# Seven products instead of eight for the second K chunk's first half in a two-layer encoder trunk

## The chip, the cores and the metric

The kernel runs on one core of one Trainium2 chip. The metric is the device time of one execution in microseconds (us). A timed value is the median of several executions. The profile comes from one further execution; its span, from the first to the last instruction, is a little shorter than that execution's time.

## What is computed

Two encoder layers on an input of 256 positions by 2048 channels, all in float32. Each layer has a mixer (pooling and grouped-query attention in layer 0, a bidirectional matrix-memory mLSTM in layer 1) and a gated feed-forward part, and each part adds its result to the residual x. The feed-forward part is the same in both layers:

```python
def conv_ffn(x, w_up, conv_w, conv_b, w_down):
    u = x @ w_up                                   # 2048 -> 2 * 5632
    up = jnp.pad(u, ((0, 0), (1, 1), (0, 0)))
    u = c[0] * up[:, :-2] + c[1] * up[:, 1:-1] + c[2] * up[:, 2:] + conv_b
    gate, val = jnp.split(u, 2, axis=-1)
    return (jax.nn.silu(gate) * val) @ w_down      # 5632 -> 2048
```

The change touches only the last product, with `w_down`, of layer 0.

## The kernel before, in words

**Precision.** Every float32 operand is split into a high part (rounded to the type F32R) and a low part, the remainder. A product is three matmuls: high by high, high by low and low by high. Weights come from DRAM in chunks of 128 by 1024 values (512 KB). `Stream` (L94 to L159) loads them on the DMA queue of SyncE (SP) into one of six buffers `w`, up to five chunks ahead. `Stream.split` (L124) makes the two parts: ScalarE (ACT) casts the high part (L135), VectorE (DVE) subtracts to get the low part (L136). There are four buffers `hl` for split chunks.

**Feed-forward.** The 44 row tiles of `w_down` (K tiles, 128 rows each) are cut into six K chunks of 4, 8, 8, 8, 8 and 8 tiles (`FCH`, L33). `up` (L993) makes one K tile of the gated activation: 64 matmuls on four weight chunks, then convolution and gate on ACT and DVE. While the tiles of one chunk are made, the `w_down` products of the chunk before it are run, one piece after each `up`; `_ffn_plan` (L1265) writes this order out, and TensorE (PE) keeps it. ACT, DVE, SP and GpSimd (POOL) are put in order by a scheduler when the program is built.

**Eight or seven products.** The 2048 output columns are two halves of two 512-column blocks. In the plain way (`down`, L1133), one call handles one block of 512 columns for all eight K tiles: 48 matmuls of 512 columns and four weight chunks. In the other way (`unit`, L1036), two K tiles, two groups of 128 positions and the two column blocks of a half form a 2 by 2 by 2 product, done in seven products in place of eight, as Strassen and Winograd do. For each pair of K tiles and each half an A unit runs four products (12 matmuls, two chunks) and a B unit three (9 matmuls, one chunk and a half). A unit called with two pairs runs twice that. The partial sums are drained from PSUM on DVE or ACT (`drain`, L1070, L1080 and L1082): four adds after a group of A units, three after a group of B units. A plain block needs two adds (L449).

`BOTH` (L35) lists the chunks for which both halves go the seven-product way. A chunk not in it does so for half 1 only, and half 0 goes through two calls of `down`. In layer 0 that was chunk 1; the last chunk is handled in a way of its own. When one half only is done so, a unit handles one pair; otherwise it handles two. `PASSES` (L39) is the order of the groups.

**Sums of weights.** The A units need four sums of `w_down` blocks for each pair and half. They are made in one of two ways (`_ffn_weights`, L1349):

- `Made`: in DRAM, by `premix` (L476). One mix is ten DMAs: four plain copies on ACT's queue and six that accumulate, on POOL's queue. Each half-tile step waits for the last matmul issued when it was written down (`paced`, L472), so mixes go along with PE. Afterwards the two chunks are loaded by SP like any weights.
- `Sum` and `Chain`: in SBUF. SP loads one chunk, POOL's queue accumulates a second onto it, and DVE makes the other two sums with two adds (L131, L132).

For a chunk that does both halves, even pairs are `Made` and odd pairs are summed in SBUF. For chunk 1 of layer 0 all four pairs of half 1 were summed in SBUF (the second condition of L1350).

**Pacing.** `Weave` (L162) keeps a program clock: each group of matmuls ticks it by its expected length (0.645 for four of `up`, 0.68 for one product). `premix(0, 26.0, 60.0, 8, ...)` (L739), called in the attention stage, starts a mix every 26 ticks up to the eighth, and every 60 afterwards; each takes five times 26 ticks. Two more mixes of layer 0, for the last chunk, are started later and faster (`LATE`, L37 and L1186). There were 16 mixes in layer 0, 14 of them from L739.

Of the kernel before, what the change touches and what calls it, by code (L numbers as in the profile page):

```python
# [31 lines left out]
FT = DFF // P  # L32
FCH = [4, 8, 8, 8, 8, 8]  # L33
CH = 8
BOTH = ((0, 2, 3, 4), (0, 1, 2, 3, 4))  # L35
LAST = (4, 4)
LATE = ((2, 3), (1, 2))  # L37

PASSES = (  # L39
    ("A1 B1 A0 B0", "A1 B1", "A1 B1 A0 B0", "A1 B1 A0 B0", "A0 A1 A1+ B0 B1 B1+"),  # L40
    ("A1 B1 A0 B0", "A1 B1 A0 B0", "A1 B1 A0 B0", "A1 B1 A0 B0", "A0 A1 A1+ B0 B1 B1+"),
)
NEG = -1.0e30
# [50 lines left out]
class Stream:  # L94
# [60 lines left out]
    def next(self):  # L155
        i = self.at
        self.ahead(i)
        self.at += 1
        return self.hl.pop(i)  # L159
# [58 lines left out]
def trunk(ctx: ExitStack, tc: tile.TileContext, gx, xT, xn, call, catt, cml, weights, mixes, out):  # L218
# [253 lines left out]
    def paced(ins):  # L472

        tc.add_manual_dep(ins.ins, last_mm[0].ins.name, now, reason="paced")

    def premix(layer, gap, late, n, which=slice(None)):  # L476

        def one(i, s0, s1, r, made):
            i += which.start or 0
            m = scratch.tile([P, 2, CH * P], F32, tag=f"m{layer}{i}", name=f"m{layer}_{i}")  # L480
            h = CH * P // 2
            steps = [(nc.scalar, m[:, 0], s0, {}), (nc.scalar, m[:, 1], r, {}), (g, m[:, 0], s1, add),
                     (g, m[:, 1, :h], m[:, 0, :h], add), (g, m[:, 1, h:], m[:, 1, :h], add)]
            for n, (eng, to, src, kw) in enumerate(steps):
                for p in range(0, P, P // 2):
                    paced(eng.dma_start(to[p : p + P // 2], src[p : p + P // 2], **kw))  # L486
                    yield (0.1, 0.6, 0.6, 0.6, 0.6)[n] * gap
            for j in range(2):
                made[j].ap = m[:, j]

        for i, e in enumerate(mixes[layer][which]):
            wv.aside(one(i, *e), min(i + 1, n) * gap + max(i + 1 - n, 0) * late)


    def attention_layer(norm, nxt):
        with ExitStack() as es:
# [239 lines left out]
            catb.extend(actp.tile([P, 8, 2, S], F32R, tag=f"B{i}", name=f"cat{i}") for i in range(2))  # L736
            wv.add(k_block(ps))
            wv.tick(0.0)
            premix(0, 26.0, 60.0, 8, slice(0, -LAST[0] // 2))  # L739
            with tc.manual_schedule(engines={mybir.EngineType.SP}):  # L740
                ps = mov_group(xx, "qproj0", after=squares)
            wv.add(q_block(ps, 0, 5.5))
# [447 lines left out]
    norms = [Norm(0), None]  # L1190
    norms[1] = Norm(1)
    attention_layer(norms[0], norms[1])
    norms.append(Norm(2))
    ffn_layer(0, norms[1], norms[2])
# [55 lines left out]
def _halves(layer, c):  # L1250

    return () if c == len(FCH) - 1 else (0, 1) if c in BOTH[layer] else (1,)

# [6 lines left out]
def _direct(layer, c, b):  # L1260

    return LAST[layer] if c == len(FCH) - 1 and b >= NB // 2 else 0


def _ffn_plan(layer):  # L1265

    slots, late, units = [[] for _ in range(FT)], [], []
    at = 1
    for c in range(len(FCH) - 1):
        at = max(at + (c == 0) * FCH[0], sum(FCH[: c + 1]))
        step = len(_halves(layer, c))
        for pas in PASSES[layer][c].split():
            k = c + pas.endswith("+")
            for j in range(0, _pairs(layer, k), step):
                units.append((pas[0], k, int(pas[1]), tuple(range(j, j + step))))
                to = slots[min(at, FT - 1)] if at <= FT else late  # L1280
                to.append(len(units) - 1)
                if step == 1 and pas[0] == "A" and j % 2:
                    to.append(("down", c, j // 2))
                at += 1
    for n, u in enumerate(units):
        first, last = (not 0 <= m < len(units) or (units[m][0], units[m][2]) != (u[0], u[2]) for m in (n - 1, n + 1))
        units[n] = u[:4] + (first, last, all(o[2] != u[2] for o in units[n + 1 :]))
    slots = [[e if isinstance(e, tuple) else units[e] for e in slot] for slot in slots]

    busy = {(u[1], j): f for f, slot in enumerate(slots) for u in slot if u[0] == "A" for j in u[3]}  # L1290
    seq, f0 = [], 0
    for c, n in enumerate(FCH):
        for i in range(n):
            seq.append(("up", c, i))
            mixes = [(busy.get((c - 1, j), 0) - f0, ("mix", c, j)) for j in range(_pairs(layer, c))]
            mixes = [(k, e) for k, e in mixes if i == max(2 * e[2] + 1, k)]

            soon = [e for k, e in mixes if c == len(FCH) - 1 and k < i]
            seq += soon + slots[f0 + i] + [e for _, e in mixes if e not in soon]
        f0 += n  # L1300
    seq += [("two", c, 0)] + [units[e] for e in late] + [("two", c, 1)]
    return seq + [("down", c, b) for b in range(2, NB)]
# [27 lines left out]
def _ffn_weights(layer, up, parts):  # L1330

    down = iter(parts[0])
    out, u, mixes = [], 0, []
    for kind, c, i, *j in _ffn_plan(layer):
        if kind == "up":
            out += up[u : u + 4]
            u += 4
        elif kind in ("down", "two"):
            n = FCH[c] // 2 - 1
            out += [next(down) for _ in range((n, n + 2)[i] if kind == "two" else (FCH[c] - _direct(layer, c, i)) // 2)]  # L1340
        elif kind != "mix":
            q0 = sum(FCH[:c]) // 2
            s0, s1, r, ba, bb = parts[1 + 5 * i : 6 + 5 * i]
            js = [q0 + e for e in j[0]]
            if kind == "B":
                last = bb[js[0] // 2]
                out += [ba[q] for q in js] + [last if len(js) == 2 else last[:, js[0] % 2 * 512 : js[0] % 2 * 512 + 512]]
                continue
            for q in js:  # L1349
                if c < len(FCH) - 1 and (q % 2 or i and c == 1 and layer == 0):  # L1350
                    out += [Sum(s0[q], s1[q]), Chain(r[q])]
                else:
                    made = [Made(), Made()]
                    mixes.append((s0[q], s1[q], r[q], made))
                    out += made
    return out, mixes
# [103 lines left out]
```

## Time and profile before

| what | value |
|---|---|
| median of 3 executions | 2159.14 us (2157.9 to 2159.89) |
| the profiled execution's own time | 2158.39 us |
| its span | 2156.6 us |
| granted TensorE clock, mean | 1.000 |
| feed-forward part of layer 0 in the span | about 263 to 967 us |
| stretch in which chunk 1 of layer 0 is multiplied by `w_down` | about 437 to 553 us |

"Busy" counts the time in which an engine has an instruction under way; for PE the ends of matmuls are modelled, so that PE at 100% may still run below its best. The DMA share is the busy time of packets over that of the 16 DMA engines. It can be somewhat over 1, where packets of several queues overlap on one engine.

### The profile page before, as it was taken

To read this page: it belongs to the slowest core of one execution; us is meant where nothing else is said; L and a number is where in the kernel's file an instruction comes from. 1 tells how busy PE (TensorE), PEld (TensorE's weight loads), DVE (VectorE), ACT (ScalarE), POOL (GpSimd) and SP (SyncE) were. 2 spreads that over 40 slices of the span, in tenths; PEclk is the share of its full clock that TensorE was granted. 3 is DMA by queue.
4 is the path that set the end of the run, shared out by engine and by line. 5 is a ranking of instruction groups with operands and counts; after the bars stand their busy time and mean duration, and the time that the engine had idled before them with its cause. 6 is when DMAs were issued, how large, how long until landed. Compare 5 with 4: busy or idle time off the path is not lost.

```text
span 2156.6 us, 32025 instructions
## 1 busy us (share of the span) xinstructions
PE 2150.5 (100%) x11400; PEld 1844.0 (86%) x11400; DVE 1746.3 (81%) x2451; ACT 1419.9 (66%) x2222; POOL 231.8 (11%) x294
## 2 busy tenths in 40 slices
PE   9999999999999999999999999999999999999999
PEld 7888888888888888889888888888888888888887
DVE  7686678887988899897777676667888998989988
ACT  7665577766777777766454544457777777777774
POOL 0022111110011110001111111111100000000000
PEclk9999999999999999999999999999999999999999
DMA  9668989897999897779887888988978988878775
GB/s 327 211 205 244 290 240 310 253 283 240 301 311 319 278 311 237 262 268 240 232 256 241 246 246 232 275 268 250 282 241 271 306 273 274 289 249 271 237 249 195
DMA packets 168164, 566.78 MB, mean 263 GB/s; under 512 B 21339, under 2 KB 23939, under 8 KB 168003
## 3 DMA queue, kind: packets, MB, share of 16 engines
q1 hardware_dynamic: 130496, 465.96, 61.5%
q0 software_dynamic: 22624, 56.90, 15.9%
q10 hardware_dynamic: 14882, 41.86, 6.0%
q8 instruction: 89, 1.46, 0.3%
q14 instruction: 73, 0.59, 0.1%
HBM read 562.51 MB, written 77.64 MB: 297 GB/s over the span
## 4 chain that ended last, share of the span: by engine, by line
PE 98%; DVE 1%; DMA 0%; issue 0%; ACT 0%; DVEq 0%
PE up L273 45%; PE pp L273 16%; PE op L273 8%; PE mv L273 4%; PE mq L273 4%; PE mk L273 4%; PE mo L273 4%; PE dn L273 4%; PE qproj L273 3%; PE vproj L273 1%; PE kproj L273 1%; PE pool L273 1%; PE av L273 1%; PE qk L273 1%; PE xt L324 0%; DVE hl L136 0%
## 5 line engine op out<-in xcount | busy, mean ns | idle before, releaser
L136 DVE TENSOR_TENSOR hl<-w,hl 128x1024 fp32r<-128x1024 f32 (+1 forms) x846 | 1017.0, 1214 | 212.0 <-ACT hl L135 209.4
L135 ACT CAST hl<-w 128x1024 fp32r<-128x1024 f32 (+1 forms) x845 | 867.0, 1045 | 429.4 <-PE up L273 123.1
L273 PE MATMUL up<-xx,hl 128*128 128x512 f32 (+1 forms) x5632 | 993.8, 337 | 0.0
L273 PEld LDWEIGHTS up<-xx,hl 128*128 128x128 f32 x5632 | 867.4, 188 | 129.8 <-DVE hl L136 0.4
L273 PE MATMUL pp<-hl,s 128*128 128x512 f32 x864 | 214.7, 390 | 0.1
L486 POOL DMA_DIRECT2D m<-m x144 | 116.4, 811 | 728.5 <-PE up L273 293.7
L273 PEld LDWEIGHTS pp<-hl,s 128*128 128x128 f32 x864 | 159.2, 188 | 31.9 <-DVE hl L136 0.9
L273 PE MATMUL pp<-hl,g 128*128 128x512 f32 x648 | 165.1, 390 | 0.0
L273 PEld LDWEIGHTS pp<-hl,g 128*128 128x128 f32 x648 | 119.1, 188 | 22.9
L439 ACT COPY tb_up<-up 128x512 f32<-128x512 f32 x88 | 51.7, 587 | 124.3 <-PE up L273 124.2
L486 POOL DMA_DIRECT2D m<-in_dn x72 | 60.9, 846 | 478.8 <-PE dn L273 149.1
L1005 DVE TENSOR_TENSOR y<-y,z 128x510 f32<-128x510 f32 x88 | 60.7, 690 | 60.3 <-ACT y L1004 60.2
L1004 ACT ACTIVATE y<-tb_up,conv 128x256 f32<-128x256 f32 x176 | 103.8, 590 | 0.0
L440 DVE TENSOR_TENSOR tb_up<-up,tb_up 128x512 f32<-128x512 f32 x88 | 60.8, 691 | 40.5 <-ACT tb_up L439 40.3
L273 PE MATMUL mk<-xx,hl 128*128 128x512 f32 (+1 forms) x512 | 92.2, 337 | 0.0
L273 PE MATMUL mq<-xx,hl 128*128 128x512 f32 (+1 forms) x512 | 92.2, 338 | 0.0
L273 PE MATMUL mv<-hl,xx 128*128 128x512 f32 (+2 forms) x480 | 91.8, 351 | 0.0
L273 PE MATMUL op<-hl,cat 128*128 128x512 f32 x384 | 91.6, 393 | 0.0
L1002 ACT ACTIVATE z<-tb_up,conv 128x256 f32<-128x256 f32 x176 | 88.5, 503 | 3.1 <-DVE tb_up L997 2.8
L273 PE MATMUL mo<-hl,xx 128*128 128x512 f32 x384 | 90.5, 391 | 0.0
L273 PE MATMUL op<-hl,mcat 128*128 128x512 f32 x384 | 89.5, 392 | 0.0
L273 PEld LDWEIGHTS mq<-xx,hl 128*128 128x128 f32 x512 | 79.3, 188 | 11.6
(233 smaller groups left out, 2180.0 us busy)
## 6 DMA issues: line engine op xcount, KB each, us to landing
w<-in_up SPq DMA_DIRECT2D x352, 512.0 KB, 5.2
w<-in_dn SPq DMA_DIRECT2D x174, 512.0 KB, 4.9
w<-in_m_in SPq DMA_DIRECT2D x124, 512.0 KB, 5.3
m<-in_dn ACTq DMA_DIRECT2D x144, 256.0 KB, 5.8
w<-m SPq DMA_DIRECT2D x72, 512.0 KB, 4.9
w<-in_a_in SPq DMA_DIRECT2D x46, 512.0 KB, 4.5
m<-in_dn POOLq DMA_DIRECT2D x72, 256.0 KB, 6.8
m<-m POOLq DMA_DIRECT2D x144, 128.0 KB, 5.4
```

Source lines behind the costliest of these rows:

```text
L135: (self.nc.vector.tensor_copy if i + c == 0 else self.nc.scalar.copy)(hl[:, 0, c : c + n], w[:, c : c + n])
L136: low = self.nc.vector.tensor_sub(hl[:, 1, c : c + n], w[:, c : c + n], hl[:, 0, c : c + n].bitcast(F32))
L273: last_mm[0] = pe.matmul(out_, lhsT, rhs, start=start, stop=stop, skip_group_check=True)
L439: a.copy(tb, ps[:, :, 1, :])
L440: v.tensor_add(tb, ps[:, :, 0, :], tb)
L486: paced(eng.dma_start(to[p : p + P // 2], src[p : p + P // 2], **kw))
L1002: a.activation(z[:, 0, j, :], u[:, j, :], AF.Copy, scale=cw(tl, 0))
L1004: a.activation(y[:, j, :], u[:, j, :], AF.Identity, scale=cw(tl, 1), bias=cw(tl, 3))
L1005: v.tensor_add(y[:, :, 1:S], y[:, :, 1:S], z[:, 0, :, 0 : S - 1])
```

## The change

Chunk 1 of layer 0 is put into `BOTH`: both its halves take seven products, and its units take two pairs at a time. Its even pairs' sums now come from DRAM and its odd pairs' from SBUF, as in the other chunks. This makes four further mixes in L739's list (18 there, 20 in layer 0), and they are placed ahead of those of chunk 2, so that the mixes of chunks 2 to 4 move back by four places. From the ninth mix on, one is started every 34 ticks instead of every 60.

```diff
-BOTH = ((0, 2, 3, 4), (0, 1, 2, 3, 4))
+BOTH = ((0, 1, 2, 3, 4), (0, 1, 2, 3, 4))
...
 PASSES = (
-    ("A1 B1 A0 B0", "A1 B1", "A1 B1 A0 B0", "A1 B1 A0 B0", "A0 A1 A1+ B0 B1 B1+"),
+    ("A1 B1 A0 B0", "A1 B1 A0 B0", "A1 B1 A0 B0", "A1 B1 A0 B0", "A0 A1 A1+ B0 B1 B1+"),
...
-            premix(0, 26.0, 60.0, 8, slice(0, -LAST[0] // 2))
+            premix(0, 26.0, 34.0, 8, slice(0, -LAST[0] // 2))
...
-                if c < len(FCH) - 1 and (q % 2 or i and c == 1 and layer == 0):
+                if q % 2 and c < len(FCH) - 1:
                     out += [Sum(s0[q], s1[q]), Chain(r[q])]
```

Around chunk 1 the order on PE becomes, after each `up` of chunk 2 (before: one pair of A or B, and after the second and the fourth a plain block):

```
A half 1 pairs 0,1 | A half 1 pairs 2,3 | B half 1 pairs 0,1 | B half 1 pairs 2,3
A half 0 pairs 0,1 | A half 0 pairs 2,3 | B half 0 pairs 0,1 | B half 0 pairs 2,3
```

## The prediction, made before the changed kernel ran

> **What bounds the kernel now.** I read the shares of the engines and the chain of waits on the page first, then the chain piece by piece, then busy time by stretch.
>
> ```profile
> span 2156.6 us, 32025 instructions
> ...
> PE 2150.5 (100%) x11400; PEld 1844.0 (86%) x11400; DVE 1746.3 (81%) x2451; ACT 1419.9 (66%) x2222; POOL 231.8 (11%) x294
> ...
> PE 98%; DVE 1%; DMA 0%; issue 0%; ACT 0%; DVEq 0%
> ```
>
> PE is the bound from end to end. A busy PE need not be at its best, so the pace has to be read from equal pieces of work. In the chain in order of time (start, length, what):
>
> ```profile
> 425.69 11.13 PE up L273 x64
> ...
> 439.56 10.88 PE dn L273 x48
> ...
> 478.17 10.88 PE dn L273 x48
> ...
> 500.19 2.05 PE pp L273 x9
> ...
> 552.93 5.45 PE pp L273 x24
> ...
> 586.11 4.09 PE pp L273 x18
> ...
> 653.82 11.14 PE up L273 x64
> ...
> 669.05 11.35 PE up L273 x64
> ```
>
> Each `up` takes 11.13 or 11.14 us, in chunk 1's stretch (one half in seven products) and in chunk 2's (both halves, from 552.93). A matmul of 512 columns takes 5.45 / 24 = 0.227 us everywhere. One piece is late, the `up` at 669.05, by 11.35 - 11.14 = 0.21 us. So removed matmuls are removed time, and what has to be asked is whether weights still come in time.
>
> ```profile
> 289.00:427.00 138.00, 138.00 (x765) 119.48 (x764) 117.68 (x163) 103.43 (x171) 20.63 (x26) 1.00 0.89 270
> 427.00:553.00 126.00, 126.00 (x674) 108.27 (x673) 103.13 (x136) 83.12 (x131) 12.03 (x15) 1.00 0.87 268
> 553.00:680.00 127.00, 127.00 (x678) 108.89 (x677) 113.26 (x150) 92.97 (x141) 16.87 (x21) 1.00 0.96 309
> 680.00:807.00 127.00, 127.00 (x680) 109.20 (x679) 114.97 (x152) 92.55 (x140) 15.35 (x19) 1.00 0.94 298
> ```
>
> The columns are PE, PEld, DVE, ACT and POOL busy (instructions), clock, DMA share and GB/s. Chunk 1 (second row) has room on every unit; chunks 2 and 3 show a stage with both halves in seven products: DVE at 90%, the DMA engines at 0.94 to 0.96, PE undisturbed but for 0.21 us.
>
> **PE's saving.** Half 0 of chunk 1 costs two plain blocks, 2 x 10.88 = 21.76 us. In seven products it costs two double A units and two double B units, 2 x 5.45 + 2 x 4.09 = 19.08 us. That is 12 matmuls fewer; 12 x 0.227 = **-2.73 us** is the term I use. Half 1 keeps its matmuls; its single units become double ones.
>
> **Vector work, covered.**
>
> ```profile
> L136 DVE TENSOR_TENSOR hl<-w,hl 128x1024 fp32r<-128x1024 f32 x832 | 1006.1, 1221 | 210.7 <-ACT hl L135 208.0
> ...
> L135 ACT CAST hl<-w 128x1024 fp32r<-128x1024 f32 x832 | 857.6, 1050 | 422.8 <-PE up L273 121.2 <-PE op L273 62.5 <-PE mo L273 32.0
> ...
> L1082 DVE TENSOR_TENSOR acc<-acc,pp 128x512 f32<-128x512 f32 x60 | 39.7, 681 | 0.0
> ...
> L449 DVE TENSOR_TENSOR x<-x,dn 128x512 f32<-128x512 f32 x18 | 11.6, 680 | 0.0
> ...
> L136 DVE TENSOR_TENSOR hl<-w,hl 128x512 fp32r<-128x512 f32 x8 | 5.4, 688 | 1.3 <-ACT hl L135 1.3
> ...
> L135 ACT CAST hl<-w 128x512 fp32r<-128x512 f32 x7 | 4.3, 621 | 4.0 <-PE up L273 2.0 <-issue 1.5 <-DMA w<-in_a_in 0.4
> ```
>
> Chunks of chunk 1 to be split: before, half 0 had 8 whole ones, half 1 had 12 whole and 4 half-wide (a single B unit loads half a chunk). After, each half has 14 whole. That is 8 whole more and 4 half-wide fewer. DVE: 8 x 1.221 - 4 x 0.688 = 7.0 us, and 7 drains in place of 4 plain adds, 7 x 0.681 - 4 x 0.680 = 2.0 us: +9.1 us. The adds of `Chain` stay, since four pairs are summed in SBUF before and after. DVE comes to (103.13 + 9.1) / 123.3 = 91% of chunk 1's stretch, and chunk 3 has 114.97 / 127 = 90.5% with PE undisturbed: I cost it at nothing. Without that cover at most the excess over chunk 3's share, some 0.6 us, would show. ACT gets 8 x 1.050 - 4 x 0.621 = 5.9 us and 16 issues of DMAs:
>
> ```profile
> L486 ACTq DMA_DIRECT2D m<-in_dn x144: 497/498/617, 58.3 to 1820.4; - x144
> L486 POOL DMA_DIRECT2D m<-m x144: 772/778/1438, 155.3 to 1868.3; - x144
> ```
>
> 16 x 0.5 = 8 us on ACT and 24 x 0.78 = 19 us on POOL, over the 500 us in which mixes run. ACT stays under 80% and POOL under 20%: nothing.
>
> **Are the sums from DRAM there in time?** A load of a sum that isn't ready would hold SP's queue, every weight load behind it, and then PE. The first eight mixes start at the same ticks as before, 26 apart, so this trace tells when they are done, whoever uses them. Chunk 1's four are now the third to the sixth.
>
> ```profile
> 364.67 0.86 POOL L121 DMA_DIRECT2D sum<-in_dn  x1 [6.58 <-DMA sum<-in_dn]
> ...
> 385.64 0.78 POOL L486 DMA_DIRECT2D m<-in_dn  x1 [4.80 <-PE up L273]
> ```
>
> In POOL's built order of before, the sixth mix's last step stands ahead of the accumulation at 364.67 and the seventh's ahead of the one at 385.64; in the built order after, the sixth's has the same place and the seventh's stands two places later. Chunk 1's products begin at 436.8, its half 0 some 60 us later, chunk 2's at 552.93. The last of L739's list ended at 208 + 6 x 60 + 130 = 698 ticks and now ends at 208 + 10 x 34 + 130 = 678, for the same unit of chunk 4. So no step is late by its pacing, and I cost this at nothing.
>
> **The DMA engines: the open cost.**
>
> ```profile
> q1 hardware_dynamic: 130496, 465.96, 61.5%
> q0 software_dynamic: 22624, 56.90, 15.9%
> q10 hardware_dynamic: 14882, 41.86, 6.0%
> ...
> w<-in_up SPq DMA_DIRECT2D x352, 512.0 KB, 5.2
> ...
> m<-in_dn ACTq DMA_DIRECT2D x144, 256.0 KB, 5.8
> ...
> m<-in_dn POOLq DMA_DIRECT2D x72, 256.0 KB, 6.8
> m<-m POOLq DMA_DIRECT2D x144, 128.0 KB, 5.4
> ```
>
> In time of all 16 engines, a MB costs 0.615 x 2156.6 / 465.96 = 2.85 us on SP's queue (q1), 3.09 on ACT's (q10) and 6.03 on POOL's (q0). A mix moves 4 x 256 KB on ACT's and 2 x 256 KB + 4 x 128 KB on POOL's queue, 1.05 MB on each: 3.24 + 6.32 = 9.56 us. A weight chunk is 0.524 MB, 1.49 us. The change adds four mixes (38.2 us) and the equal of 28 - 22 = 6 chunks (8.9 us). Where does it fall? A slot of `up` and a double A unit ticks 16 x 0.645 + 8 x 0.68 = 15.76 in 11.13 + 5.45 = 16.58 us, so 60 ticks are 63.1 us and 34 are 35.8. From the ninth mix on, mixes take 9.56 / 35.8 = 0.267 of the engines, not 9.56 / 63.1 = 0.151: +0.116. Chunk 1's chunks add 8.9 / 126 = 0.07. The stretches become 0.87 + 0.116 + 0.07 = **1.06** and 0.96 + 0.116 = **1.08**; the other 9 us lie about them (0.89 to some 0.93, 0.94 to 0.97). How full can they get? Stretches of 25 us:
>
> ```profile
> 0.00:25.00 25.00, 23.40 (x91) 18.88 (x92) 18.60 (x37) 18.12 (x29) 0.73 (x9) 1.00 0.95 368
> 200.00:225.00 25.00, 25.00 (x119) 20.71 (x118) 15.17 (x20) 13.94 (x24) 4.81 (x6) 1.00 1.05 317
> 350.00:375.00 25.00, 25.00 (x137) 21.55 (x136) 22.83 (x30) 17.96 (x29) 4.03 (x5) 1.00 1.02 315
> 625.00:650.00 25.00, 25.00 (x138) 21.58 (x137) 23.19 (x33) 16.90 (x27) 4.08 (x5) 1.00 1.03 336
> 650.00:675.00 25.00, 25.00 (x133) 21.20 (x132) 20.26 (x28) 19.58 (x32) 5.48 (x7) 1.00 1.00 328
> ```
>
> 1.05 is the most. The two rows at 625 to 675, at 1.03 and 1.00, end in the one late `up`. There ACT waited for weights, in the list of waits of 553 to 807:
>
> ```profile
> ACT hl L135 <- DMA w<-in_up: 4.6, 5, 2.6
> ```
>
> So the engines, now full in spots, would be full for some 250 us. The cost from both sides: nothing, if it is as at 350 to 375 (full, no late piece); 0.06 x 126 + 0.08 x 127 = 17.7 us, if all above 1.00 delays PE. A share counts waiting within a packet too: 0.95 moved 368 GB/s in the first row, where 0.87 moved 268 at chunk 1, so that sums of shares overstate. I take the nearest row, 0.21 us lost in 50 us at 1.00 to 1.03, for 253 us: 1.06, say **+1.0 us**.
>
> **The sum.** -2.73 + 1.0 = -1.7 us: 2158.39 becomes 2156.7 in the profiled execution (its span lies 1.8 below its time). The median of the runs is 0.75 above that execution, so the forecast for the median is **2157.4 us**, -0.08%. About 0.2% (4.3 us) is what a measurement of this kernel can tell from no change; the whole saving on PE, 0.13%, is below it.
>
> **The rivals.**
>
> *Everything is hidden.* The shares overstate the load; PE runs as evenly as in chunk 3's stretch. For: 350 to 375. Against: 669.05. 2159.1 - 2.7 = 2156.4.
>
> *The gain is eaten.* The engines hold 1.05 over the whole stretch, as at 200 to 225, and the rest delays PE: 0.01 x 126 + 0.03 x 127 = 5.1 us, 2161.5.
>
> *Slower: weights late in the stretch from 427 to 680.* Accumulating DMAs and weight loads share the engines. If they hold only what 625 to 650 shows, 1.03, the rest is 0.03 x 126 + 0.05 x 127 = 10.1 us, 2166.5. It decides against the change from a lost 2.73 us on, and shows as slower by over 0.2% from 7.1 us on, at a ceiling of about 1.04. The worst place is from 616 on, where the first of the two fast late mixes runs beside the others. For: 0.21 us there already. Against: the late mix runs in that place now as well, and mixes are paced by PE, so that they wait when PE does. The Trainium skill, in HBM Reference, Specifications (TRN2), gives about 358 GB/s for a core; by it, an estimate from 309 GB/s and 25 more for the denser mixes, with the mixes' writes to DRAM counted as well, the stage of chunk 2 would already be over the limit. This trace speaks against so low a limit: its first row moved 368 GB/s. The same skill, in DMA: Bandwidth & Descriptors, Issuing engines are not separate DMA queues, says that the transfers of all queues interleave on the same 16 engines; by that the loads do pay for the mixes, and the rows at 625 to 675 agree.
>
> *The change does something else.* The scheduler may place DVE's and ACT's work otherwise and remove more than it costs. There is little to remove: 0.21 us in this part. For over 0.2% faster, -4.3 us, something outside the steps above would have to move.
>
> **How the numbers follow.** Forecast (0.5 to 2.5 us lost) 0.46; everything hidden 0.18; gain eaten (2.5 to 7 us lost) 0.14; slower 0.18, at 2166.5 or beyond in half of it; something else, faster, 0.04. The first three lie within 0.2%: same 0.78, slower 0.18, faster 0.04. The range goes from everything hidden less 1 us of scatter (the three runs span 2.0 us), 2155.4, to 2164.5, which takes in the eaten gain and the lower part of the slower case; some 0.14 is left out above and 0.04 below.
>
> **What would show it.** In the chain after, chunk 1's stretch should have no `dn` of 48 matmuls, four pieces of 5.45 and four of 4.09, and `up` at 11.14; the start of chunk 3's products should be 2.7 us earlier less what was lost. The DMA share from 427 to 680 should be 1.0 or over. If `up` pieces are longer there and ACT's L135 waits for DMA, the slower rival holds; if they wait for L136 instead, my cover on DVE was wrong. If SP waits for a DMA of a mix, the lateness that I cost at nothing was wrong. A share well under 1.0 would make my sum of shares wrong.

## The result and the profile after

| kernel | median | lowest to highest | ratio to before, 95% interval |
|---|---|---|---|
| before | 2159.14 us | 2157.9 to 2160.58, 7 runs | |
| changed | 2165.8 us | 2162.3 to 2170.32, 7 runs | 1.0032 [1.0022, 1.0042] |

The changed kernel is slower by 6.7 us, and its runs scatter over 8 us where those of before scatter over 2.7. With the 2.73 us that PE was to save, 6.7 + 2.7 = 9.4 us are lost in a median run. The profiled execution is the fastest of the seven, 2162.30 us against 2158.39 before; it lost 3.9 + 2.7 = 6.6 us. So the trace shows a mild case; where the slower runs lost the rest isn't recorded.

The page of the changed kernel, the span, the busy times and the chain by engine:

```profile
span 2160.5 us, 32121 instructions
...
PE 2150.2 (100%) x11388; PEld 1840.7 (85%) x11388; DVE 1754.6 (81%) x2458; ACT 1426.3 (66%) x2226; POOL 250.7 (12%) x318
...
PE 95%; DVE 3%; DMA 1%; issue 1%; ACT 0%; ACTq 0%; DVEq 0%
```

There are 12 matmuls fewer, and PE is on the chain for 95%, not 98%: DVE, DMA and issue (time in which the profile shows no wait) have got in. The same stretches as in the prediction (columns PE, PEld, DVE, ACT, POOL busy, clock, DMA share, GB/s):

```profile
289.00:427.00 138.00, 138.00 (x762) 119.05 (x761) 117.52 (x164) 104.35 (x173) 22.85 (x29) 1.00 0.91 284
427.00:553.00 126.00, 126.00 (x676) 108.27 (x675) 112.86 (x146) 91.16 (x137) 20.32 (x26) 1.00 0.99 322
553.00:680.00 127.00, 122.96 (x650) 103.65 (x649) 107.49 (x141) 89.24 (x135) 22.98 (x29) 1.00 1.01 321
680.00:807.00 127.00, 126.17 (x674) 108.07 (x674) 114.59 (x151) 92.05 (x140) 17.64 (x22) 1.00 0.94 299
```

In chunk 1's own stretch, the second row, PE is busy all the time. PE idles in the third row, 127.00 - 122.96 = 4.0 us, and a little in the fourth. The chain in order of time (start, length, what):

```profile
423.09 5.45 PE pp L273 x24
428.54 11.15 PE up L273 x64
...
508.78 11.14 PE up L273 x64
...
538.69 0.49 ACT y L1004
...
554.87 9.27 DMA w<-in_dn
...
574.64 11.14 PE up L273 x64
...
652.26 15.48 DMA w<-in_dn
...
667.82 1.06 ACT hl L135
668.90 1.24 DVE hl L136
...
671.62 0.43 ACTq L486
...
687.47 1.23 DVE hl L136
...
690.17 11.14 PE up L273 x64
```

Up to 535 the pieces are as short as before, and the plain blocks of 10.88 us are gone. Then the chain leaves PE three times. From 538.69 it runs over ACT and DVE to the load of a weight chunk, 9.27 us at 554.87, and returns over DVE. From 649 it goes to a second load, 15.48 us at 652.26, and returns through the cast on ACT and the subtraction on DVE. The third time, from 671.62 to 688.75, it stays on ACT and DVE and there is no load in it. The list of waits from 553 to 700 shows the side of those who wait (in total, times, longest):

```profile
ACT hl L135 <- DMA w<-in_dn: 8.9, 5, 2.5
DVE w L131 <- DMA w<-in_dn: 6.2, 3, 4.7
PEld pp L273 <- DVE hl L136: 5.8, 5, 1.3
ACT hl L135 <- DMA w<-in_up: 5.1, 7, 1.1
```

The worst place is where the first fast late mix runs beside the others, 616 to 680. Queues (packets, MB, share) and loads (count, size, median us to landing) there, before:

```profile
q0 software_dynamic: 1166, 3.01, 25.5%
...
w<-in_up SPq DMA_DIRECT2D x16, 512.0 KB, 8.0
w<-in_dn SPq DMA_DIRECT2D x8, 512.0 KB, 9.2
```

and in the changed kernel:

```profile
q0 software_dynamic: 1411, 3.63, 31.2%
...
w<-in_up SPq DMA_DIRECT2D x15, 512.0 KB, 10.7
w<-in_dn SPq DMA_DIRECT2D x8, 512.0 KB, 9.1
```

POOL's accumulating queue takes 31% of the engines for 3.63 MB, and the loads for `up` land 2.7 us later at the median; those for `dn` don't, 9.1 us against 9.2. PE waits for L136, and L136 in its turn stands behind chunks that came late. Whether late chunks or DVE's own work start this, the trace alone can't tell: DVE is on the chain for 3%, the loads for 1%. The experiments have to.

### The profile page after: what moved, and what is told of

Same layout as the page of the kernel before. It is cut to its first block, busy times and chain, and to the rows that moved or that the text cites. A ratio compares the mean times of both kernels' runs of the same rounds, so it can differ in the third digit from the quotient of the medians.

```text
span 2160.5 us, 32121 instructions
## 1 busy us (share of the span) xinstructions
PE 2150.2 (100%) x11388; PEld 1840.7 (85%) x11388; DVE 1754.6 (81%) x2458; ACT 1426.3 (66%) x2226; POOL 250.7 (12%) x318
## 3 DMA queue, kind: packets, MB, share of 16 engines
HBM read 574.04 MB, written 86.03 MB: 306 GB/s over the span
## 4 chain that ended last, share of the span: by engine, by line
PE 95%; DVE 3%; DMA 1%; issue 1%; ACT 0%; ACTq 0%; DVEq 0%
PE up L273 43%; PE pp L273 16%; PE op L273 8%; PE mv L273 4%; PE mq L273 4%; PE mk L273 4%; PE mo L273 4%; PE qproj L273 3%; PE dn L273 3%; DVE hl L136 1%; DMA w<-in_dn 1%; PE kproj L273 1%; PE vproj L273 1%; PE pool L273 1%; PE av L273 1%
## 5 line engine op out<-in xcount | busy, mean ns | idle before, releaser
L136 DVE TENSOR_TENSOR hl<-w,hl 128x1024 fp32r<-128x1024 f32 (+1 forms) x850 | 1023.2, 1216 | 205.0 <-ACT hl L135 201.7
L273 PE MATMUL pp<-hl,s 128*128 128x512 f32 x912 | 227.5, 390 | 3.3 <-DVE hl L136 3.2
L486 POOL DMA_DIRECT2D m<-m x160 | 129.6, 815 | 796.0 <-PE up L273 319.4
L273 PEld LDWEIGHTS pp<-hl,s 128*128 128x128 f32 x912 | 167.9, 188 | 38.6 <-DVE hl L136 5.7
L273 PE MATMUL pp<-hl,g 128*128 128x512 f32 x684 | 174.5, 390 | 1.1 <-DVE hl L136 0.8
L273 PEld LDWEIGHTS pp<-hl,g 128*128 128x128 f32 x684 | 125.8, 188 | 26.2 <-DVE hl L136 1.1
L486 POOL DMA_DIRECT2D m<-in_dn x80 | 68.6, 859 | 404.2 <-PE dn L273 137.2
```

What stands on the lines that cost most here:

```text
L136: low = self.nc.vector.tensor_sub(hl[:, 1, c : c + n], w[:, c : c + n], hl[:, 0, c : c + n].bitcast(F32))
L273: last_mm[0] = pe.matmul(out_, lhsT, rhs, start=start, stop=stop, skip_group_check=True)
```

## The experiments

Two theories were set against each other. TRAFFIC: the 16 DMA engines are too full with mixes, so weight loads land late. VECTOR: DVE has too much to split and to drain. All times are medians; "lost" is the difference to the kernel before as timed along with that run, plus 2.73 us where half 0 of chunk 1 is done in seven products.

| run | seven products for both halves | mixes | median, us | ratio, 95% interval | lost, us |
|---|---|---|---|---|---|
| changed | yes | 20, every 34 | 2165.8 | 1.0032 [1.0022, 1.0042] | 9.4 |
| e1 | no | as changed, 4 unread | 2169.47 | 1.0049 [1.0036, 1.0061] | 10.5 |
| e2 | yes, sums in SBUF | as before | 2159.24 | 1.0000 [0.9991, 1.0009] | 3.0 |
| e3 | yes | earlier | 2159.3 | 1.0003 [0.9994, 1.0012] | 3.1 |
| e4 | no | 16, every 34 | 2160.33 | 1.0006 [0.9998, 1.0015] | 1.4 |
| e5 | yes | first late one slower | 2160.97 | 1.0012 [1.0003, 1.0021] | 4.7 |
| e6 | yes | earlier, none late | 2157.04 | 0.9991 [0.9982, 1.0000] | 0.8 |
| e7 | no | e1, unread ones plain | 2169.86 | 1.0052 [1.0038, 1.0066] | 10.9 |
| e8 | yes | still earlier, none late | 2156.42 | 0.9990 [0.9981, 0.9999] | 0.2 |
| e9 | no | e1, unread ones at 515 to 740 us | 2169.3 | 1.0046 [1.0033, 1.0059] | 10.2 |
| e10 | no | e9, unread ones plain | 2163.55 | 1.0019 [1.0010, 1.0028] | 4.5 |
| e11 | no | e8's | 2159.86 | 1.0007 [0.9998, 1.0016] | 0.8 |
| e12 | yes | every 34, none late | 2161.89 | 1.0014 [1.0005, 1.0023] | 5.5 |

### e1: the mixes without the products

```diff
-            premix(0, 26.0, 60.0, 8, slice(0, -LAST[0] // 2))
+            premix(0, 26.0, 34.0, 8, slice(0, -LAST[0] // 2))
...
+        if l == 0:
+            m[2:2] = [e[:3] + ([Made(), Made()],) for e in m[2:6]]
         mixes.append(m)
```

> The kernel before (plain blocks for half 0 of chunk 1, four pairs of half 1 summed in SBUF) with the changed kernel's mixes: four further mixes of which nobody reads the result, in the same four places of the list, and one mix every 34 ticks from the ninth on. The result is the reference's. TRAFFIC theory (the 16 DMA engines are too full with mixes, weight loads land late): the loss of the changed kernel without its gain. That loss is 2165.8 - 2159.1 + 2.7 = 9.4 us, so about 2168 us, 2164 to 2171. VECTOR theory (the further splits and drains on DVE make the split chunks late): DVE's work is that of before, so 2158.5 to 2160 us.

2169.47 us: the loss without the gain, 10.5 us, about 1 us more than the 9.4 of the changed kernel. DVE had no more to do than before. VECTOR falls as the main cause; TRAFFIC holds. The stretch 616 to 680 of this run:

```profile
616.00:680.00 64.00, 59.76 (x308) 49.17 (x307) 50.12 (x66) 42.01 (x66) 12.15 (x15) 1.00 1.02 319
```

PE is missing 4.2 us in it, and DVE, with 50.12 of 64 us, is less busy than in the same stretch before (57.34) and in the changed kernel (53.41): it waits as well.

### e2: the products without further mixes

The further condition for chunk 1 is widened to both its halves, and the pacing is that of before.

```diff
-                if q % 2 and c < len(FCH) - 1:
+                if c < len(FCH) - 1 and (q % 2 or c == 1 and layer == 0):
```

> The changed kernel with seven products for both halves of chunk 1, but all its pairs summed in SBUF, so no further mixes, and 60 ticks between mixes as before. TRAFFIC theory: the mixes' load is that of before, so most of the 2.7 us is kept: 2156 to 2158 us. VECTOR theory: DVE has the changed kernel's splits and drains and 8 more adds of 0.68 us, 5.5 us, which makes it 95% of chunk 1's stretch: as late as the changed kernel or later, 2165 us or more.

2159.24 us, between the two: 6.6 us better than the changed kernel, and yet the 2.73 us are eaten. DVE got 8 more adds than in the changed kernel, so VECTOR's 2165 us and more are refuted; TRAFFIC's 2156 to 2158 us are missed too. The chain of this run from 480 to 530, and two of its waits from 490 to 530, show waits behind which the rest can have gone:

```profile
490.46 9.09 DMA sum<-in_dn
...
512.46 12.07 DMA w<-in_up
```

```profile
POOL sum L121 <- DMA sum<-in_dn: 17.4, 3, 8.3
...
DVE w L131 <- DMA sum<-in_dn: 3.5, 1, 3.5
```

A sum in SBUF is two transfers one after the other into one of three buffers. With eight such pairs in chunk 1, DVE waits 3.5 us for one of them, and behind this wait stand the splits of the chunks that PE needs. So this variant pays, at least in part, in lateness of its own sums; a weight load, 12.07 us at 512.46, is on its chain as well, and the two weren't separated.

### e3: mixes in the attention stage

```diff
-            premix(0, 26.0, 34.0, 8, slice(0, -LAST[0] // 2))
+            premix(0, 20.0, 42.0, 10, slice(0, -LAST[0] // 2))
```

> The changed kernel with its mixes moved to the attention stage, where the DMA share is 0.53 to 0.80 from 75 to 200 us: a mix every 20 ticks for the first ten, every 42 afterwards (before the edit 26 for eight, then 34). TRAFFIC theory: mixes take 9.56 / 44 = 0.22 of the engines from 400 us on instead of 0.27, and end some 40 us earlier: the loss falls from 9.4 us to 2 to 6 us, 2158.5 to 2162.5 us. VECTOR theory: DVE's work is unchanged: 2164 to 2167 us.

2159.3 us: 6.3 of the 9.4 us come back by moving the same DMAs, with DVE's work unchanged.

### e4: the kernel before with denser mixes

> The kernel before with one edit, 34 ticks in place of 60 between its 14 mixes: as many mixes as before, denser from about 290 us on and ended at 542 ticks, some 590 us, so ahead of the fast late mix at 616 us. TRAFFIC theory: shares of 0.98 to 1.08 up to 590 us, less afterwards: 0 to 3 us lost, 2159 to 2162 us; if it is the amount of mixes together with the late mix that costs, nothing is lost. VECTOR theory: 2159 us.

Its edit is the first of e1's. 2160.33 us, an interval that holds 1. Its list of mixes ended later than the 590 us expected: the last step was issued on POOL at 623.56 us, the first POOL step of the late mix at 642.96. So a dense stretch ahead of the late mix costs little, and the four mixes more, which carry the density on through the late mix, come with the other 9 us of e1.

### e5 and e12: the late mix

e5 gives the first late mix 24 ticks in place of 12. e12 takes the late ones out of their place and sets them at the end of the list.

```diff
-LATE = ((2, 3), (1, 2))
+LATE = ((), (1, 2))
...
-            premix(0, 26.0, 34.0, 8, slice(0, -LAST[0] // 2))
+            premix(0, 26.0, 34.0, 8)
```

> The changed kernel with one edit: the first of the two late mixes, which starts at about 616 us, takes 5 x 24 ticks in place of 5 x 12. TRAFFIC theory, with the late mix as the place that matters (PE's losses of the profiled executions lie at 640 to 690 us for the greater part): the late mix's share falls from 0.15 to 0.075 of the engines there, and some 5 of the 9.4 us lost come back: 2159.5 to 2163 us. TRAFFIC theory without that (the density from 427 to 680 us alone matters): 2164.5 to 2167 us.

> The changed kernel with one edit: no late mixes, its two last ones stand at the end of the list instead, at the unchanged 26 and 34 ticks. TRAFFIC theory with the late mix as the place that matters most: as e5_late_mix_slower or a little better, 2158.5 to 2161 us, with what is lost at 565 to 575 us left over. If moving mixes into the attention stage is what counts: 2164 us or more.

2160.97 us and 2161.89 us: about half of the loss, 4.7 and 3.9 us, is the late mix's. e12 came out 0.9 us above its range, with 5.5 us still lost: what is left without the late mix is more than I had allowed for.

### e6 and e8: earlier and none late

e6 is e12 with `premix(0, 20.0, 40.0, 10)`, e8 with `premix(0, 18.0, 46.0, 12)`.

> The changed kernel with all 20 mixes of layer 0 in the list that starts in the attention stage (no late ones), a mix every 20 ticks for the first ten and every 40 afterwards. TRAFFIC theory: mixes take 9.56 / 42 = 0.23 of the engines, evenly, with nothing fast on top at 616 us, and the loss falls to 0 to 1.5 us: 2156.3 to 2158 us, faster than the kernel before. If density alone matters and not the late mix, as e3_mixes_earlier: 2159 to 2160 us.

> e6_earlier_no_late with a mix every 18 ticks for the first twelve and every 46 afterwards: 9.56 / 48 = 0.20 of the engines after some 330 us, at the price of 0.50 before. TRAFFIC theory: 2156.3 to 2157.5 us, no later than e6_earlier_no_late, unless the attention stage, denser now, loses something itself (PE's pieces from 100 to 260 us would show it).

2157.04 and 2156.42 us. e8 keeps 2.6 of the 2.73 us and is the fastest of all kernels here, 0.1% below the one before, with an interval that leaves out 1 only just. Four kernels, with the late mix in place or not and the list early or not, make a table of what is lost: late mix, list not early 9.4 (changed); no late mix, list not early 5.5 (e12); late mix, list early 3.1 (e3); no late mix, list early 0.8 (e6, which has 40 ticks where e3 has 42). e8's stretch from 616 to 680 and its chain:

```profile
616.00:680.00 64.00, 64.00 (x343) 54.97 (x343) 58.48 (x78) 46.91 (x72) 8.07 (x10) 1.00 0.97 309
```

```profile
428.47 11.15 PE up L273 x64
...
572.35 11.14 PE up L273 x64
...
651.20 11.14 PE up L273 x64
...
666.43 11.14 PE up L273 x64
677.56 5.45 PE pp L273 x24
683.01 11.13 PE up L273 x64
...
730.05 11.13 PE up L273 x64
```

PE is undisturbed at a share of 0.97, with DVE at 58.48 / 64 = 91%. So DVE, at the load that the prediction called covered, is covered. This profiled execution, 2155.15 us, is the fastest of its eleven.

### e11: e8's pacing on the kernel before

> The kernel before with e8_earlier_sparser's pacing alone: all 16 mixes from the attention stage on, every 18 ticks for twelve, then every 46, none late. TRAFFIC theory: the kernel before lost 0.21 us to the late mix and nothing else, so there is nothing to gain: 2158.5 to 2159.5 us, and e8_earlier_sparser's 2.6 us are those of the 12 matmuls. If earlier mixes gain something by themselves: 2156 to 2158 us.

2159.86 us, an interval that holds 1 and a median 0.4 us above its range: the pacing gains nothing by itself, so e8's gain is that of the 12 matmuls. In its trace PE is missing 1.75 us from 289 to 427, where e8 at the same pace misses nothing; why isn't known.

### e7, e9 and e10: does accumulation count?

e7 is e1 with the four unread mixes' accumulations made plain copies. e9 is e1 with the unread mixes 13th to 16th in the list (`m[12:12]` in place of `m[2:2]`); e10 is e9 with theirs made plain.

```diff
-        def one(i, s0, s1, r, made):
+        def one(i, s0, s1, r, made, add=add):
...
-            m[12:12] = [e[:3] + ([Made(), Made()],) for e in m[2:6]]
+            m[12:12] = [e[:3] + ([Made(), Made()], {}) for e in m[2:6]]
```

> e1_traffic_only with the four unread mixes' accumulating DMAs made plain copies: the same ten DMAs, queues and bytes, no addition (what they write is read by nobody; the result is the reference's). If it is the engines' time that counts, and accumulation is what makes a MB on POOL's queue cost 6.03 us and not about 3, a mix costs 6.5 us and not 9.56, and the loss falls from 10.5 to 3 to 6 us: 2162 to 2165 us. If bytes, or the number of DMAs on the queues, count: 2168 to 2171 us as e1_traffic_only.

> As e1_traffic_only, the kernel before with the changed kernel's rate of mixes, but the four unread mixes stand 13th to 16th in the list, so that their own DMAs run from about 515 to 740 us, where PE's losses lie, and not before 370 us. TRAFFIC theory: the same DMAs run at the same times, only for other data, so as e1_traffic_only: 2168 to 2171 us.

> e9_traffic_in_place with the accumulating DMAs of the four unread mixes made plain copies (nobody reads what they write). If it is engine time that counts and accumulation costs 6.03 us a MB where a plain copy costs about 3, the mixes of 515 to 740 us load the engines by 0.18 in place of 0.27, and most of the 10.5 us lost comes back: 2160 to 2164 us. If bytes or the number of DMAs count: 2168 to 2171 us, as e9.

e7, 2169.86 us against 2162 to 2165 expected, looks as if accumulation cost nothing. But it was set up badly: the third to sixth mixes run before 370 us, where PE loses nothing, so what is saved on them can't come back. Its trace does give the price. From 160 to 270 us, POOL's queue in e1 and then in e7:

```profile
q0 software_dynamic: 1872, 4.85, 25.3%
```

```profile
q0 software_dynamic: 1744, 4.85, 19.1%
```

The same MB take a quarter less of the engines' time when part of them is copied and not added.

e9 and e10 put them where the losses are: 2169.3 and 2163.55 us. The same DMAs with the same bytes on the same queues, without the addition, give back 5.7 of 10.2 us. In the stretch 616 to 680, e9 first, then e10:

```profile
q0 software_dynamic: 1396, 3.62, 32.4%
...
w<-in_up SPq DMA_DIRECT2D x13, 512.0 KB, 12.0
w<-in_dn SPq DMA_DIRECT2D x8, 512.0 KB, 12.9
```

```profile
q0 software_dynamic: 1182, 3.50, 25.6%
...
w<-in_up SPq DMA_DIRECT2D x14, 512.0 KB, 10.7
w<-in_dn SPq DMA_DIRECT2D x8, 512.0 KB, 10.7
```

About as many MB take 32.4% or 25.6% of the engines, and the weights land 1.3 to 2.2 us earlier. So it is the engines' time that counts, more than the bytes that the profile counts.

## Why the prediction was wrong

**What bounds the kernel; PE's saving: right.** The plain blocks are gone, the pieces measure 5.45 and 4.09 us, and the medians of e8 and before differ by 2.58 of the 2.73 us. The chain shows it without that scatter: the same `up` begins at 653.82 us before and at 651.20 in e8, 2.62 us earlier.

**Vector work, covered: right.** DVE did 112.86 of 126 us in chunk 1's stretch, 90% (91% forecast), with PE undisturbed there. e1 and e8 settle that this work isn't the main cause: the loss comes without DVE's further work, and it goes with that work in place.

**Sums there in time: right.** The profile after shows PE's delays behind weights from `in_dn` and `in_up`; ACT's waits for loads of mixes are 0.5 us where those for `in_dn` are 8.9. SP, whose wait for a mix was to be the sign of lateness, waits 1.1 us for DMAs of mixes in the first 1000 us, and 2.8 us before the change.

**The DMA engines: the step that failed.** The mechanism was the one named, and so was the worst place, from 616 on: the engines are full, and weights come late. It stood as the rival with a chance of 0.18 and 2166.5 us, and the median is 2165.8. What failed is the size of the term: "I take the nearest row, 0.21 us lost in 50 us at 1.00 to 1.03, for 253 us: 1.06, say +1.0 us". Measured, the term is 9.4 us.

The loss was taken to grow with the length of the full stretch. It doesn't. Set beside the same `up` pieces in e8, those of the changed kernel begin 0.1 us later at 428.54, 2.3 us later at 574.64, and 7.2 us later at 690.17 as well as at 737.22. So the profiled execution loses in two short places: 2.2 us ahead of 575, and 4.9 us from 638 to 690. Nor does the share say where: at 0.99 PE was missing nothing from 427 to 553, and at the same 0.99 it was missing 1.6 us from 553 to 616 (the third row of the table above, in two parts):

```profile
553.00:616.00 63.00, 61.40 (x329) 52.13 (x328) 54.08 (x71) 43.60 (x66) 10.09 (x13) 1.00 0.99 312
616.00:680.00 64.00, 61.55 (x324) 51.52 (x323) 53.41 (x71) 45.64 (x69) 12.88 (x16) 1.00 1.03 330
```

The second place is the late mix's. The term treated the stretch as one, though this mix takes 9.56 us of the engines' time in some 64 us there, before the change as well, and now on top of the denser mixes. In the trace of e5, where it takes twice as long, the 4.9 us are 1.0, and in that of e12, where it isn't in this place, 2.3. The first place is left in these two, with 3.1 and 3.2 us, and it needs more than mixes: e1 and e9, which have the mixes without the further chunks of chunk 1, lose about 1 us there, and e8, which has these chunks without the dense mixes, loses nothing. Whether it is the loads of these chunks or their splits that meet the mixes there wasn't separated.

That the rival's 2166.5 us came so near is partly luck. Its 10.1 us were what a sum of shares has above 1.03, spread over both stretches, 3.8 us of it in chunk 1's. Nor were its signs as I had given them: the `up` pieces kept their 11.14 us and the products were late, and PE's waits for L136 stand beside ACT's for DMAs, so that the two signs didn't tell the theories apart. e1 did.

The sums of shares, 1.06 and 1.08, came out as 0.99 and 1.01: they did overstate, as the prediction said, and I drew comfort from that. But the share says little once it is near 1. No 25 us of before have more than 1.05, and the same 1.03 from 616 to 680 goes with 2.5 us of missing PE time in the changed kernel and 4.9 in e9. What differs is the landing times. For the loads of `up` and of `dn` in this stretch they are 6.0 and 7.1 us in e8, where nothing is lost, 8.0 and 9.2 before, with one piece 0.21 us late, 10.7 and 9.1 in the changed kernel, and 12.0 and 12.9 in e9. The trace of before had them: 5.2 us for `in_up` over the span, and 8.0 from 616 to 680. That row is the best sign there was of how little was left, and the prediction didn't use it. That the loss sets in once the split chunks kept ready are used up fits this, but no run measured how many were left.

The Trainium skill's statement that the transfers of all queues interleave on the same engines (DMA: Bandwidth & Descriptors, Issuing engines are not separate DMA queues) is borne out by e1: four mixes that nobody reads, on other queues than the weights', bring 9 of its 10.5 us (e4, the same without them, loses 1.4).

The Trainium skill gives some 358 GB/s for a core in HBM Reference, Specifications (TRN2), and says there that a core streaming alone measures well above this share. The trace agrees: slices of 1.6 us from 616 to 680 of the changed kernel move up to 425 GB/s. And GB/s don't rank the losses: e10 moves 332 GB/s from 616 to 680 and PE is missing 1.7 us there, e9 moves 315 and it is missing 4.9.

```profile
616.00:680.00 64.00, 59.07 (x299) 47.85 (x298) 50.34 (x66) 41.37 (x64) 12.18 (x15) 1.00 1.03 315
```

```profile
616.00:680.00 64.00, 62.34 (x326) 52.11 (x325) 53.83 (x71) 45.70 (x71) 10.98 (x16) 1.00 0.99 332
```

(e9 above, e10 below.) More bytes, less engine time, less loss. One reservation: the pages of e9 and e10 give the same MB read from and written to DRAM, 570.89 and 86.03, so that what an addition reads besides isn't told in them.

**What stays open.** Why runs of the changed kernel scatter over 8 us wasn't settled. Nor was it tried whether a seventh weight buffer would ride out the stretch, or what a lighter load on DVE would do: e1 excludes DVE's further work as the main cause, not that DVE, busy as it is before the change, makes each delay longer. Whether the loads wait for bandwidth in memory, for the engines or for their turn among the queues can't be told from these runs.

## What to carry to other kernels

Where transfers run in the background of a bound engine, read their price from the stage with the least reserve, and read the reserve from landing times; a mean share near 1 hardly moved here. A change that saves the bound engine's time and adds background transfers should move these to a stage with room as part of the same change: here that made the difference between 6.7 us lost and 2.6 us won. A small delay in the trace of before can mark an edge: here 0.21 us stood before a loss of 9.4, out of proportion to the load added.

## What the runs showed of the hardware

A MB on POOL's queue, where nearly all DMAs accumulate, took 6.03 us of the 16 engines' time in the trace of before, against 2.85 on SP's queue and 3.09 on ACT's, where all are plain. That the addition, and not POOL's queue alone, has a large part in it is shown by runs that move about the same bytes on POOL's queue with some of the additions left out: e7 against e1 (19.1% of the engines against 25.3% for 4.85 MB) and e10 against e9 (25.6% for 3.50 MB against 32.4% for 3.62). And issuing the same mixes earlier, with nothing else changed than their order and pace, moved the kernel's time by 9 us (the changed kernel 2165.8 us, e8 2156.42).
